# Building the first stage of a projection as a pipeline over feature tiles

## The chip, the cores and the metric

The kernel runs on one core of one Trainium2 chip. The metric is the device time of one execution in microseconds (us), the median of the runs. A core has TensorE (PE: matrix products, with PEld for the loading of their weights), VectorE (DVE), ScalarE (ACT), GpSimd (POOL) and SyncE (SP), which in this kernel issues every DMA transfer. Each engine works off its own list of instructions in order; engines wait for each other by semaphores.

## The reference

Two layers of a diffusion block over 512 tokens (256 latent, 256 context) of 2048 features. The change lies in the head of the even layer, where each token's features are normalised, scaled and shifted, and projected:

```python
shift, scale, gate = jnp.split((s_lat @ ada_w[layer] + ada_b[layer])[:, None, :], 3, axis=-1)   # s_lat = silu(c)
h = rms_norm(x, pre_g[layer]) * (1.0 + scale) + shift
...
hc = rms_norm(ctx, pre_g[layer]) * (1.0 + scale_c) + shift_c      # the same with c_ctx
...
a_v, a_g, b_x, b_b, b_c, b_g = jnp.split(h @ w_in, idx, axis=-1)  # w_in: 2048 x 6144
```

`rms_norm` divides a token by the root of the mean of its squares and multiplies by `pre_g`. So the scale of a feature is a sum over 2048 rows of `ada_w`, and the division by the root is one number per token (called r below), the same for all features. What follows (pooling and convolution, an output projection, the odd layer's gated recurrence) is not touched.

## The kernel before

Features lie on the 128 partitions, 16 feature tiles k of 128 features, and the 512 tokens lie along the free axis, latent and context tokens in the two halves v. A float32 product is made as three products of two-part values: `split` has ScalarE round a value to its high part (L131) and VectorE subtract it for the low part (L132), and `mm3` (L171) issues high x high, high x low and low x high. The low half of a weight, `wlo`, is therefore the last thing that a product waits for.

The first stage makes 7 of the 48 output tiles at once (G0 = 7), one PSUM bank each: `main0(k)` (L337) multiplies a weight of 128x896 (`evg`, 448 KB) by feature tile k into all seven, 21 products of 512 columns, and 16 such passes complete them. Ahead of it the program runs in this order:

- The parameters (L69, 128x344 values, 172 KB) and x, four transfers of 1024 KB (L86), are loaded. ScalarE squares each feature tile of x (L324) and TensorE sums the squares over the partitions (L325, `colsum_mm`); this ends in `r0`, and in `rb0`, r spread over all partitions (`to_rows`).
- The scale columns, silu(c) @ ada_w, are made by TensorE with `col_mm` (L206, products of 32 output rows at L212) from pieces `adaraw` of two 1024 KB transfers each (`ada_raw`, L345), 4 feature tiles to a unit (the first one in two halves of two). VectorE transposes the sums (L230) and `ada_end` adds the bias and multiplies by `pre_g`: `mod`.
- `make_h0` (L352) makes h for a unit's feature tiles: VectorE multiplies x by `mod` and r (L357), ScalarE rounds h to its high half (L360), VectorE makes the low half (L361).

The passes `main0` lie between the units (L376 to L390). The last four lie between the shift columns, of which half is made by TensorE as above and half by VectorE: `ada_dve` (L260) multiplies and sums pieces of a transposed weight, `adat`, of 128x1024 (512 KB) with a row `srow` of silu(c) (loaded and put through SiLU by `load_srow`, L255). `step(n)` does n pieces, two reductions each (L270), one for c and one for c_ctx. `loads` (L115) asks for each piece one step ahead of its use, from a tag `raw2` of two buffers; the weights of the products have a tag `raw` of three, freed by the low half.

After `main0(15)`, `keep` (L408) copies the seven tiles out of PSUM on ScalarE, and `proj_tile` (L176) makes tiles 7 to 11 one at a time, each of two weights of 128x1024 and 48 products, with `step(2)` at each half. All tiles up to the 12th are made of h without the shift; `add_shift` (L413) adds it to h during the last of them, and a bias is made for the tiles that lacked it.

Of the kernel before, what the change touches and what calls it, by code (L numbers as in the profile page):

```python
# [7 lines left out]
F32 = mybir.dt.float32  # L8
# [7 lines left out]
P = 128  # L16
D = 2048
# [30 lines left out]
def block_kernel(ctx: ExitStack, tc: tile.TileContext, par, xt, invcnt, poolw, ada, adat, crow, evg, evb, ev, evo,  # L48
# [36 lines left out]
    for k in range(0, KT, 4):  # L85
        nc.sync.dma_start(xr[k // 8][:, k % 8:k % 8 + 4, :], xt[:, k:k + 4, :])  # L86
# [173 lines left out]
    def ada_dve(units):  # L260

        parts = [(l, t, 4 * u + i, half) for l, t, u in units for i in range(4) for half in range(2)]
        srcs = [adat[ADAT[l, t], n, :, half * 1024:half * 1024 + 1024] for l, t, n, half in parts]
        for (l, t, n, half), raw in zip(parts, loads(srcs)):
            i = n % 4
            if not i and not half:
                sums = a0.tile([P, 2, 4, 2], F32, name="asum", bufs=2)
            for v in range(2):
                junk = a0.tile([P, 1024], BF16, name="ajunk")
                tc.keep_in_program_order(V.tensor_tensor_reduce(  # L270
                    junk, raw, srow[:, v, half * 1024:half * 1024 + 1024], 1.0, sums[:, 0, i, v:v + 1] if half else 0.0,
                    op0=ALU.mult, op1=ALU.add, accum_out=sums[:, half, i, v:v + 1]))
            if half and i == 3:
                ada_end(l, t, n - 3, sums[:, 1])
            yield
# [45 lines left out]
    st0 = aux_ps([P, 1, P], "stps")  # L321
    for k in range(KT):
        sq = tmp512("sq")
        S.activation(sq, xr[k // 8][:, k % 8, :], AF.Square)  # L324
        colsum_mm(st0[:, 0, :], sq, k == 0, k == KT - 1)  # L325
    sxx = cst.tile([P, 4], F32, name="sxx")
    V.tensor_copy(sxx, colsum_end(st0)[:, 0, :])
    r0 = cst.tile([P, 4], F32, name="r0")
    rsqrt_mean(r0, sxx)
# [5 lines left out]


    def main0(k):  # L337

        hh, hl = act0(k)
        whi, wlo = weights()  # L340
        for g in range(G0):
            w = slice(g * P, g * P + P)
            mm3(grp[g], whi[:, w], wlo[:, w], hh, hl, k == 0, k == KT - 1)

# [7 lines left out]
    def make_h0(ks):  # L352
        for k in ks:
            h = xr[k // 8][:, k % 8, :]
            for v in range(2):
                c = slice(v * SEQ, v * SEQ + SEQ)
                V.scalar_tensor_tensor(h[:, c], h[:, c], mod[:, 0, 1, k, v:v + 1], rb0[:, c],  # L357
                                       op0=ALU.mult, op1=ALU.mult)
            hh, hl = act0(k)
            S.copy(hh, h)  # L360
            V.tensor_tensor(hl, h, hh.bitcast(F32), op=ALU.subtract)  # L361


    for t in h0[0] + h0[1]:
        GP.memset(t[:, 0, 0:1].bitcast(F32), 0.0)
    raws = [ada_raw(0, 1, 0, s) for s in range(2)]
    for s in range(2):
        acc = aux_ps([P, 64], "adaps")
        for g in range(4):
            col_mm(acc, s_pad, raws[s][:, g, :], g, 4)  # L370
        ada_pe_end(0, 1, 2 * s, acc)
        if s == 0:
            rb0, _ = to_rows(r0, a0.tile([P, 512], F32, name="rb0", tag="a2k"))
            grp = [mm_ps() for _ in range(5)] + [aux_ps([P, 512], "mmx") for _ in range(G0 - 5)]
        make_h0((2 * s, 2 * s + 1))
    for u in range(1, 4):  # L376
        acc = aux_ps([P, P], "adaps")
        for s in range(2):
            if u == 1 and s == 0:
                main0(0)  # L380
                main0(1)
            if u == 3 and s == 0:
                load_srow()
            raw = ada_raw(0, 1, u, s)
            for g in range(4):
                col_mm(acc, s_pad, raw[:, g, :], 4 * s + g)
            for k in range(2, 4) if (u, s) == (1, 0) else () if u == 1 else range(4 * u - 4 + 2 * s, 4 * u - 2 + 2 * s):
                main0(k)
        ada_pe_end(0, 1, 4 * u, acc)
        make_h0(range(4 * u, 4 * u + 4))  # L390

    job = ada_dve([(0, 0, u) for u in range(2, 4)])

    for u in range(2):
        acc = aux_ps([P, P], "adaps")
        for s in range(2):
            raw = ada_raw(0, 0, u, s)
            for g in range(4):
                col_mm(acc, s_pad, raw[:, g, :], 4 * s + g)
            main0(12 + 2 * u + s)  # L400
            step(1 + u)
        ada_pe_end(0, 0, 4 * u, acc)
# [5 lines left out]
    def keep(i, o):  # L408
        d = pend[i // 8][:, i % 8, :]
        S.copy(d, o)  # L410
        return d

    def add_shift(ks):  # L413
        for k in ks:
            hh, hl = act0(k)
            h = xr[k // 8][:, k % 8, :]
# [6 lines left out]
    done = [keep(i, grp[i]) for i in range(G0)]  # L423
    while len(done) < NPRE - 1:
        t = mm_ps()
        proj_tile(t, act0, lambda half: step(2))
        done.append(keep(len(done), t))
# [771 lines left out]
```

## Time and the profile before

| | |
|---|---|
| median of 3 runs | 1687.82 us (1687.19 to 1688.19) |
| profiled execution, its own time | 1686.03 us |
| its span, first to last instruction | 1684.3 us |
| mean granted clock of TensorE | 0.991 of full speed |
| TensorE busy | 1641.8 us, 97% of the span |
| VectorE busy | 1195.4 us, 71% |
| ScalarE busy | 597.5 us, 35% |
| DMA engines, mean busy share | 53.0% of 16 engines |

Busy time and waits are taken from one profiled execution, so its own time, 1686.03 us, is what they add up to; it lies 1.8 us under the median of the runs. The share of TensorE is an average over all stages. What a change in the first stage does is read from that stage's own stretch of time and from the waits in it.

### The profile page before, as it was taken

The page shows a single profiled execution, that of the slowest core. Times are in us where ns is not written, and L with a number is a line of the kernel's source. Part 1 is how long each engine was busy: PE and PEld are TensorE (multiplying, and loading weights), DVE is VectorE, ACT ScalarE, POOL GpSimd, SP SyncE. Part 2 cuts the span into 40 slices and gives each one's busy share as a digit, 9 for nine tenths or more (in the row PEclk, how much of TensorE's full clock was granted, in tenths as well). Part 3 has the DMA queues.
Part 4 walks back from the last instruction along what each step waited for, and adds up shares of the span by engine and source line. Part 5 has one row for each costly group of instructions (what it writes and reads, how often), then busy time and mean ns, then how long its engine had stood idle before and what let it go on. Part 6 is the DMA issues. An engine that isn't in the chain of part 4 may idle for free.

```text
span 1684.3 us, 23062 instructions
## 1 busy us (share of the span) xinstructions
PE 1641.8 (97%) x8878; PEld 1355.5 (80%) x8878; DVE 1195.4 (71%) x2079; ACT 597.5 (35%) x944; POOL 79.4 (5%) x154
## 2 busy tenths in 40 slices
PE   6999999999999999997999999999999999999997
PEld 4777778888888888885788888888888888888886
DVE  3458977977777778876995863878548773666854
ACT  4323533322222233332443432443334442343543
POOL 0000000000000000004100000000100000000000
PEclk9999999999999999998999999999999999999999
DMA  9987455666665686643376533636325333333453
GB/s 359 354 311 229 162 184 168 195 194 195 190 197 191 194 294 199 199 151 110 91 176 185 184 113 100 211 111 204 121 93 189 118 113 100 120 106 113 175 186 126
DMA packets 98046, 295.28 MB, mean 175 GB/s; under 512 B 26000, under 2 KB 26128, under 8 KB 96272
## 3 DMA queue, kind: packets, MB, share of 16 engines
q1 hardware_dynamic: 97936, 293.82, 53.0%
q8 instruction: 69, 1.13, 0.3%
q14 instruction: 41, 0.34, 0.1%
HBM read 289.58 MB, written 4.19 MB: 174 GB/s over the span
## 4 chain that ended last, share of the span: by engine, by line
PE 91%; DVE 5%; DMA 3%; issue 1%; ACT 0%; POOL 0%; SPq 0%; DVEq 0%; POOLq 0%; ACTq 0%
PE mmps L173 19%; PE mmps L174 19%; PE mmps L172 19%; PE mmps L191 6%; PE mmps L952 3%; PE mmps L954 3%; PE mmps L953 3%; PE mmps L192 3%; DMA adaraw<-ada_dram 1%; PE adaps L212 1%; PE mmps L1060 1%; PE mmps L1061 1%; PE mmps L1059 1%; DVE wlo L132 1%; PE mmx L173 1%
## 5 line engine op out<-in xcount | busy, mean ns | idle before, releaser
L131 ACT CAST whi<-raw 128x1024 fp32r<-128x1024 f32 (+3 forms) x328 | 335.7, 1025 | 842.6 <-PE mmps L173 547.5
L132 DVE TENSOR_TENSOR wlo<-raw,whi 128x1024 fp32r<-128x1024 f32 (+3 forms) x328 | 388.8, 1187 | 291.3 <-ACT whi L131 283.8
L172 PE MATMUL mmps<-h,whi 128*128 128x512 f32 x1216 | 477.9, 394 | 8.0 <-ACT h L710 6.5
L173 PE MATMUL mmps<-h,whi 128*128 128x512 f32 x1216 | 477.0, 392 | 3.8 <-DVE h L711 3.7
L174 PE MATMUL mmps<-h,wlo 128*128 128x512 f32 x1216 | 475.2, 391 | 3.5 <-DVE wlo L132 3.5
L172 PEld LDWEIGHTS mmps<-h,whi 128*128 128x128 f32 x1216 | 229.4, 189 | 59.5 <-ACT h L710 7.1
L174 PEld LDWEIGHTS mmps<-h,wlo 128*128 128x128 f32 x1216 | 229.2, 188 | 53.3 <-DVE wlo L132 4.4
L173 PEld LDWEIGHTS mmps<-h,whi 128*128 128x128 f32 x1216 | 229.8, 189 | 52.1 <-DVE h L711 5.0
L191 PE MATMUL mmps<-h,whi 128*128 128x512 f32 x496 | 177.8, 401 | 0.0
L192 PE MATMUL mmps<-h,wlo 128*128 128x256 f32 x496 | 139.2, 281 | 0.2 <-DVE wlo L132 0.2
L270 DVE CUSTOM_DVE_ANT_0 ajunk<-raw,srow,asum 128x1024 bf16<-128x1024 f32 x104 | 133.2, 1281 | 2.7 <-DMA raw<-adat_dram 1.2
L270 DVE CUSTOM_DVE_ANT_0 ajunk<-raw,srow 128x1024 bf16<-128x1024 f32 x104 | 126.9, 1220 | 2.6 <-DMA raw<-adat_dram 1.5
L191 PEld LDWEIGHTS mmps<-h,whi 128*128 128x128 f32 x496 | 93.1, 188 | 22.9 <-issue 0.5
L952 PE MATMUL mmps<-whi,h 128*128 128x512 f32 x256 | 100.1, 391 | 0.0
L954 PE MATMUL mmps<-wlo,h 128*128 128x512 f32 x256 | 99.8, 390 | 0.0
L953 PE MATMUL mmps<-whi,h 128*128 128x512 f32 x256 | 99.8, 390 | 0.0
L172 PE MATMUL mmps<-yin,whi 128*128 128x512 f32 x256 | 99.6, 389 | 0.0
L173 PE MATMUL mmps<-yin,whi 128*128 128x512 f32 x256 | 99.6, 389 | 0.0
L174 PE MATMUL mmps<-yin,wlo 128*128 128x512 f32 x256 | 99.6, 389 | 0.0
L192 PEld LDWEIGHTS mmps<-h,wlo 128*128 128x128 f32 x496 | 93.6, 189 | 1.2 <-DVE wlo L132 0.5
L954 PEld LDWEIGHTS mmps<-wlo,h 128*128 128x128 f32 x256 | 48.0, 188 | 10.1
L174 PEld LDWEIGHTS mmps<-yin,wlo 128*128 128x128 f32 x256 | 48.0, 188 | 10.1
(271 smaller groups left out, 1967.5 us busy)
## 6 DMA issues: line engine op xcount, KB each, us to landing
raw<-odz_dram SPq DMA_DIRECT2D x118, 512.0 KB, 3.3
raw<-adat_dram SPq DMA_DIRECT2D x104, 512.0 KB, 4.6
raw<-ev_dram SPq DMA_DIRECT2D x82, 512.0 KB, 4.3
adaraw<-ada_dram SPq DMA_DIRECT2D x24, 1024.0 KB, 9.2
raw<-ada_dram SPq DMA_DIRECT2D x36, 512.0 KB, 4.4
raw<-evo_dram SPq DMA_DIRECT2D x32, 512.0 KB, 4.5
raw<-odi_dram SPq DMA_DIRECT2D x32, 512.0 KB, 3.3
raw<-odo_dram SPq DMA_DIRECT2D x32, 512.0 KB, 3.4
```

The source lines that it names most:

```text
L131: S.copy(hi[:, 0:n], raw[:, 0:n])
L132: V.tensor_tensor(lo[:, 0:n], raw[:, 0:n], hi[:, 0:n].bitcast(F32), op=ALU.subtract)
L172: T.matmul(o, whi, xhi, start=first, stop=False)
L173: T.matmul(o, whi, xlo, start=False, stop=False)
L174: T.matmul(o, wlo, xhi, start=False, stop=last)
L191: T.matmul(o, whi, xhl, start=first, stop=False)
L192: T.matmul(o[:, 0:SEQ], wlo, xhl[:, 0, :], start=False, stop=last)
L212: T.matmul(acc[32 * j:32 * j + 32, :], vec[:, k, :], rv[:, i, j, :], start=k == 0, stop=k == KT - 1, tile_position=(0, 32 * j))
L270: tc.keep_in_program_order(V.tensor_tensor_reduce(junk, raw, srow[:, v, half * 1024:half * 1024 + 1024], 1.0, sums[:, 0, i, v:v + 1] if ha ...
L952: T.matmul(o, xh[:, c], hi[:, w], start=k == 0, stop=False)
L953: T.matmul(o, xl[:, c], hi[:, w], start=False, stop=False)
L954: T.matmul(o, xh[:, c], lo[:, w], start=False, stop=k == KT - 1)
```

## The change

The first stage becomes a pipeline over small units of feature tiles: (0), (1), and then pairs (2, 3) to (14, 15). For each feature tile the scale columns have a 1024 KB transfer of their own (`adas`, in longer rows) and x one of 256 KB (`fetch`). h is made of x and `mod` alone, without r (`scale0`); r multiplies the outputs when they are kept (`keep`, now on VectorE), and `norm_job` multiplies x by `mod` and r later, for `add_shift`. The squares are added up on VectorE (`squares`) and summed over partitions once, near the end. The order of the stage is written out by hand (`manual_schedule`: what stands there keeps the order of the code on every engine). The shift columns made by TensorE lie between the last two passes; the steps on VectorE begin three units in, two to a unit, where `load_srow` now stands too.

```diff
-    for k in range(0, KT, 4):
-        nc.sync.dma_start(xr[k // 8][:, k % 8:k % 8 + 4, :], xt[:, k:k + 4, :])
...
-    st0 = aux_ps([P, 1, P], "stps")
-    for k in range(KT):
-        sq = tmp512("sq")
-        S.activation(sq, xr[k // 8][:, k % 8, :], AF.Square)
-        colsum_mm(st0[:, 0, :], sq, k == 0, k == KT - 1)
...
+    one_b = cst.tile([P, KT], F32, name="one_b")
+    V.tensor_scalar(one_b, ada_b[:, 0, 1, :], 1.0, None, op0=ALU.add)
+    ssq = a0.tile([P, 512], F32, name="ssq", tag="a2k")
...
+    def fetch(ks):
+        raw = big_tile([P, 2, D], F32, "adaraw")
+        for i, k in enumerate(ks):
+            nc.sync.dma_start(raw[:, i, :], adas[k])
+        for k in ks:
+            nc.sync.dma_start(xk(k), xt[:, k, :])
+        return raw
+    def scale0(ks, raw):
+        n = len(ks)
+        acc = aux_ps([P, 32 * n], "adaps")
+        rv = raw.rearrange("p n (k j i) -> p n k j i", k=KT, j=4)
+        for i in range(KT):
+            for j in range(4):
+                T.matmul(acc[32 * j:32 * j + 32, :].rearrange("p (n i) -> p n i", n=n), s_pad[:, i, :],
+                         rv[:, 0:n, i, j, :], start=i == 0, stop=i == KT - 1, tile_position=(0, 32 * j))
+        tr = transposed(acc, 32 * n, a0)
+        for i, k in enumerate(ks):
+            m = mod[:, 0, 1, k, :]
+            V.tensor_scalar(m, tr[:, 32 * i:32 * i + 2], one_b[:, k:k + 1], pre_g[:, 0, k:k + 1], op0=ALU.add,
+                            op1=ALU.mult)
+        for i, k in enumerate(ks):
+            m = mod[:, 0, 1, k, :]
+            hh, hl = act0(k)
+            for v in range(2):
+                c = slice(v * SEQ, v * SEQ + SEQ)
+                S.activation(hh[:, c], xk(k)[:, c], AF.Copy, scale=m[:, v:v + 1])
+                V.scalar_tensor_tensor(hl[:, c], xk(k)[:, c], m[:, v:v + 1], hh[:, c].bitcast(F32), op0=ALU.mult,
+                                       op1=ALU.subtract)
+    def squares(ks):
+        for k in ks:
+            sq = tmp512("sq") if k else ssq
+            S.activation(sq, xk(k), AF.Square)
+            if k:
+                V.tensor_tensor(ssq, ssq, sq, op=ALU.add)
...
+    def main0(k, gs=range(G0)):
...
+    def shift0(s, acc, raw):
+        for g in range(4):
+            col_mm(acc, s_pad, raw[:, g, :], 4 * s + g)
...
+    units = [(0,), (1,)] + [(k, k + 1) for k in range(2, KT, 2)]
+    del order[-KT:]
+    first_w = {}
+    with tc.manual_schedule():
+        job = iter(())
+        raws, w_raws = [], []
+        for ks in units[:2]:
+            raws.append(fetch(ks))
+            w_raws.append([load(evg[k]) for k in ks])
+        for i, ks in enumerate(units):
+            prev = units[i - 1] if i else ()
+            if len(prev) == 2:
+                main0(prev[0])
+            elif prev:
+                main0(prev[0], range(4))
+            scale0(ks, raws[i])
+            for k, raw in zip(ks, w_raws[i]):
+                first_w[k] = split(raw, G0 * P)
+            if 0 < i < len(units) - 1:
+                w_raws.append([load(evg[k]) for k in units[i + 1]])
+            if i + 2 < len(units):
+                raws.append(fetch(units[i + 2]))
+            squares(ks)
+            if i == 3:
+                load_srow()
+                job = ada_dve([(0, 0, u) for u in range(2, 4)])
+            if len(prev) == 2:
+                step(2)
+                main0(prev[1])
+            elif prev:
+                main0(prev[0], range(4, G0))
...
+        ahead()
+        acc = aux_ps([P, P], "adaps")
+        raw = [ada_raw(0, 0, 0, s) for s in range(2)]
+        shift0(0, acc, raw[0])
+        raw.append(ada_raw(0, 0, 1, 0))
+        main0(KT - 2)
+        shift0(1, acc, raw[1])
+        raw.append(ada_raw(0, 0, 1, 1))
+        ada_pe_end(0, 0, 0, acc)
+        st0 = aux_ps([P, 1, P], "stps")
+        colsum_mm(st0[:, 0, :], ssq)
+        sxx = cst.tile([P, 4], F32, name="sxx")
+        V.tensor_copy(sxx, colsum_end(st0)[:, 0, :])
+        r0 = cst.tile([P, 4], F32, name="r0")
+        rsqrt_mean(r0, sxx)
+        main0(KT - 1, range(4))
+        rb0, _ = to_rows(r0, a0.tile([P, 512], F32, name="rb0", tag="a2k"))
+        acc = aux_ps([P, P], "adaps")
+        shift0(0, acc, raw[2])
+        main0(KT - 1, range(4, G0))
+        shift0(1, acc, raw[3])
+        ada_pe_end(0, 0, 4, acc)
+        step(1)
+    manual = False
...
-    raws = [ada_raw(0, 1, 0, s) for s in range(2)]
-    for s in range(2):
-        acc = aux_ps([P, 64], "adaps")
-        for g in range(4):
-            col_mm(acc, s_pad, raws[s][:, g, :], g, 4)
-        ada_pe_end(0, 1, 2 * s, acc)
-        if s == 0:
-            rb0, _ = to_rows(r0, a0.tile([P, 512], F32, name="rb0", tag="a2k"))
-            grp = [mm_ps() for _ in range(5)] + [aux_ps([P, 512], "mmx") for _ in range(G0 - 5)]
-        make_h0((2 * s, 2 * s + 1))
...
-        S.copy(d, o)
...
+        V.tensor_tensor(d, o, rb0, op=ALU.mult)
...
+    def norm_job():
+        for k in range(KT):
...
+                V.scalar_tensor_tensor(xk(k)[:, c], xk(k)[:, c], mod[:, 0, 1, k, v:v + 1], rb0[:, c], op0=ALU.mult,
+                                       op1=ALU.mult)
+            if k % 2:
+                yield
...
+    norms = norm_job()
     while len(done) < NPRE - 1:
         t = mm_ps()
-        proj_tile(t, act0, lambda half: step(2))
+        proj_tile(t, act0, lambda half: (step(1), next(norms, None)))
...
-    w = a["ada_w"][0, :, D:D + 512].reshape(4, 4, P, 2, 2, 4, 32)
-    ada[0, 1, 0] = w.transpose(3, 0, 2, 1, 5, 4, 6).reshape(8, P, 1024)
+    adas = a["ada_w"][0, :, D:2 * D].reshape(KT, P, KT, 4 * 32).transpose(2, 1, 0, 3).reshape(KT, P, D)
```

What this makes of the queues is seen in two places. **The first place** is SyncE's list around one unit. Before, around the last unit of scale columns and the first two of shift columns (`raw` is a weight of the products, `raw2` a piece of the reduction, `adaraw` a piece of columns, and a number behind a name tells one buffer's use from the next):

```order
L104 DMA raw_941<-evg_dram 128x896
L348 DMA adaraw_990<-ada_dram 128x2x1024 x2
L104 DMA raw_1025<-evg_dram 128x896
L104 DMA raw2_1052<-adat_dram 128x1024
L104 DMA raw2_1054<-adat_dram 128x1024
L348 DMA adaraw_1061<-ada_dram 128x2x1024 x2
L104 DMA raw_1096<-evg_dram 128x896
L104 DMA raw2_1123<-adat_dram 128x1024
```

And in the changed kernel, SyncE's list over the same unit of work, in the middle of the loop (feature tiles 8 and 9 are fetched after the weights of tiles 6 and 7, and the next unit's weights follow):

```order
L105 DMA raw_694<-evg_dram 128x896
L105 DMA raw_696<-evg_dram 128x896
L350 DMA adaraw_698<-adas_dram 128x2048 x2
L352 DMA xr_70<-xt_dram 128x512 x2
L105 DMA raw2_709<-adat_dram 128x1024
L105 DMA raw2_715<-adat_dram 128x1024
L105 DMA raw_848<-evg_dram 128x896
L105 DMA raw_850<-evg_dram 128x896
```

Before, two pieces of the reduction stand together behind one weight, ahead of the columns; now the pieces `raw2_709` and `raw2_715` stand behind two weights, two transfers of columns and two of x. **The second place** is VectorE's list where the steps of the reduction begin. Before, in the shift units (`ajunk` is the reduction's unused output, `asum` its sums, and the one-column row behind a reduction reads the sum out; the `raw2` in a row tells which piece it needs):

```order
L361 TENSOR_TENSOR h0_196<-xr_70,h0_194 128x512 x2
L132 TENSOR_TENSOR wlo_1028<-raw_1025,whi_1027 128x896
L270 ISA ajunk_1057,asum_1056<-raw2_1052,srow_88 128x1024
...
L270 ISA ajunk_1059,asum_1056<-raw2_1052,srow_88 128x1024
...
L132 TENSOR_TENSOR wlo_1099<-raw_1096,whi_1098 128x896
L270 ISA ajunk_1125,asum_1056<-raw2_1054,srow_88,asum_1056 128x1024
...
L230 STREAM_TRANSPOSE adatr_1129<-adaps_989 128x128
```

And in the changed kernel, VectorE's list from the low halves of tile 6's weight and the next to the transpose for tiles 8 and 9:

```order
L133 TENSOR_TENSOR wlo_687<-raw_533,whi_686 128x896
L133 TENSOR_TENSOR wlo_691<-raw_535,whi_690 128x896
L383 TENSOR_TENSOR ssq_95<-ssq_95,sq_703 128x512
L383 TENSOR_TENSOR ssq_95<-ssq_95,sq_706 128x512
L271 ISA ajunk_711,asum_556<-raw2_561,srow_84 128x1024
...
L271 ISA ajunk_713,asum_556<-raw2_561,srow_84 128x1024
...
L271 ISA ajunk_717,asum_556<-raw2_709,srow_84,asum_556 128x1024
...
L271 ISA ajunk_719,asum_556<-raw2_709,srow_84,asum_556 128x1024
...
L231 STREAM_TRANSPOSE adatr_828<-adaps_763 128x64
L367 TENSOR_SCALAR mod_83<-adatr_828,one_b_93,pt_67 128x2 x2
L375 SCALAR_TENSOR_TENSOR h0_88<-xr_70,mod_83,h0_86 128x256 x4
```

Before, one step lies between two low halves, and no h waits behind it: all of h0 was made ahead of the first step. Now two steps lie ahead of the transpose that h of the next two tiles needs, and the second of them reads `raw2_709`, the piece that stands behind the fetch in SyncE's list above.

## Rows read from the trace of the kernel before

**Rows 1.** The page's top: span, and each engine's busy time, share, instructions.

```profile
span 1684.3 us, 23062 instructions
...
PE 1641.8 (97%) x8878; PEld 1355.5 (80%) x8878; DVE 1195.4 (71%) x2079; ACT 597.5 (35%) x944; POOL 79.4 (5%) x154
```

**Rows 2.** Three windows: length, busy PE/PEld/DVE/ACT/POOL, granted clock, DMA share, GB/s.

```profile
0.00:27.77 27.77, 14.60 (x386) 8.51 (x387) 7.53 (x31) 14.69 (x25) 3.34 (x15) 0.94 0.95 374
27.77:131.04 103.27, 100.74 (x978) 80.32 (x978) 52.05 (x96) 33.29 (x43) 0.53 (x1) 0.98 0.86 325
131.04:200.00 68.96, 65.99 (x282) 53.96 (x283) 66.53 (x124) 29.10 (x53) 0.00 (x0) 0.98 0.60 194
```

**Rows 3.** TensorE in order of time: start, busy us, what, [idle before <-releaser].

```profile
16.69 1.10 PE L212 MATMUL adaps<-adaraw,s_pad 128*32 128x64 f32 x64
...
67.29 0.50 PE L172 MATMUL mmps<-h,whi 128*128 128x512 f32 x1
...
77.03 1.96 PE L212 MATMUL adaps<-adaraw,s_pad 128*32 128x128 f32 x64
...
131.04 0.50 PE L174 MATMUL mmps<-h,wlo 128*128 128x512 f32 x1 [0.53 <-DVE wlo L132]
...
194.73 0.60 PE L174 MATMUL mmps<-h,wlo 128*128 128x512 f32 x1 [2.97 <-DVE wlo L132]
```

**Rows 4.** The chain that ended last, in order of time: start, us, what.

```profile
28.54 0.43 PE mmps L173
...
31.41 0.23 PE mmps L172
```

**Rows 5.** ScalarE in order of time.

```profile
6.53 2.19 ACT L324 ACTIVATE sq<-xr 128x512 f32<-128x512 f32 x4 [0.18 <-DMA xr<-xt_dram]
...
14.10 2.19 ACT L324 ACTIVATE sq<-xr 128x512 f32<-128x512 f32 x4 [0.32 <-DMA xr<-xt_dram]
...
26.69 1.92 ACT L131 CAST whi<-raw 128x896 fp32r<-128x896 f32 x2 [0.62 <-DMA raw<-evg_dram]
...
67.58 1.92 ACT L258 ACTIVATE srow<-srow 128x2048 f32<-128x2048 f32 x1
...
175.70 10.11 ACT L420 ACTIVATE h<-xr,mod 128x256 fp32r<-128x256 f32 x25
```

**Rows 6.** SyncE's waits before 135 us: total us, times, longest.

```profile
SPq L104 <- DVE asum L270: 19.0, 4, 8.4
SPq L104 <- DVE wlo L132: 18.8, 6, 5.4
```

**Rows 7.** VectorE in order of time.

```profile
22.80 0.25 DVE L230 STREAM_TRANSPOSE adatr<-adaps 128x64 f32<-128x64 f32 x1 [3.09 <-PE adaps L212]
...
28.23 0.17 DVE L224 TENSOR_SCALAR mod<-mod 128x4 f32<-128x4 f32 x1
...
32.43 2.09 DVE L132 TENSOR_TENSOR wlo<-raw,whi 128x896 fp32r<-128x896 f32 x2
...
68.39 3.26 DVE L357 SCALAR_TENSOR_TENSOR xr<-xr,mod,rb 128x256 f32<-128x256 f32 x8
...
102.19 1.28 DVE L270 CUSTOM_DVE_ANT_0 ajunk<-raw,srow,asum 128x1024 bf16<-128x1024 f32 x1
```

**Rows 8.** The page's transfers: count, KB each, median us from issue to landing.

```profile
raw<-odz_dram SPq DMA_DIRECT2D x118, 512.0 KB, 3.3
```

**Rows 9.** SyncE's issues in order of time: start, us, transfer, count.

```profile
90.67 1.52 SPq L348 DMA_DIRECT2D adaraw<-ada_dram  x2
...
92.29 0.41 SPq L104 DMA_DIRECT2D raw<-evg_dram  x1
```

**Rows 10.** Landings of transfers issued at 92.29, 103.25 and 101.16 us.

```profile
raw<-evg_dram SPq DMA_DIRECT2D x1, 448.0 KB, 7.6
...
raw<-evg_dram SPq DMA_DIRECT2D x1, 448.0 KB, 11.4
...
raw<-adat_dram SPq DMA_DIRECT2D x1, 512.0 KB, 4.4
```

## What was predicted, before the changed kernel had run

> **What bounds the kernel now.** I read the page first: TensorE is busy 1641.8 us of a span of 1684.3 [rows 1], so a change can only save time where TensorE stands, and costs all that it makes it stand. Next the stages [rows 2]: up to 27.77 us TensorE is busy 14.60 us, on column sums and on the products that make the scale columns; the first product of the projection starts there. From 27.77 to 131.04 it is busy 100.74 of 103.27 us. The two later losses are in its order of time [rows 3]: a wait that ends at 131.04, where the first full-width tile (call it tile 7) gets its weights, and one that ends at 194.73, where VectorE is late with the low half of a weight (2.97 us). The chain shows the clock's two levels by the time one 512-column product takes in it: 0.43 us at 1.2 GHz, 0.23 at 2.4 [rows 4].
>
> In this stage the transfers are the second resource. Four x loads of 1024 KB let the squares start from 6.53 to 14.10 us [rows 5], so 1024 KB per 2.52 us, 406 KB/us. SyncE issues every transfer in the order of the program, and the waits of its queue show what that costs: before 135 us it stood 19.0 us for the reduction of L270 and 18.8 us for low halves of weights [rows 6].
>
> **Start: what is removed.** The squares no longer stand ahead of the products, and 1024 KB of scale columns now serve one feature tile. The first scale product needs parameters (172 KB), the pool's counts (256), and 1024 KB: 1452 KB. The first square before waited for 1196 KB until 6.53 [rows 5]; 256 KB more at 406 make 7.2. 64 products of 32 columns: the row of 32 products with 64 columns (64 records) took 1.10 us [rows 3], so 1.1 to 2.2 at the high level, times 1.9 at the low: I take 2.4, to 9.6. Then the chain of a unit: transpose 0.25, a short operation per tile 0.17, the high halves on ScalarE 0.40 per 256 columns, the cast of a weight 0.96, its low half 1.05 [rows 5, 7]. The first main product (a pass `main0`) starts at about 11.7, **16 us earlier**.
>
> **Up to unit 3 TensorE paces.** A pass of 21 products is half of 77.03 less 67.29, so 4.87 us [rows 3]; a scale product of two tiles, 64 products of 64 columns, is twice 1.10. Unit 0's twelve products at mostly the low level end at 16.3; scale product 1.5, the other nine 2.0; then a wait on unit 1's chain of about 1 us, twelve products, the scale product of tiles 2 and 3 to 25.8, nine products; a wait of 1.6 (one tile gives too little cover for the chain), main product of tile 2, the scale product of 4 and 5 to 36.7. The chain of two tiles, from the end of the scale product to the first low half of a weight, is 0.25 + 0.34 + 4 x 0.40 + 0.96 + 1.05, 4.2 us: the low half of tile 4 stands at 40.9.
>
> **What the change adds: VectorE waits for a transfer that stands behind the fetch.** In the loop, two steps of the reduction stand on VectorE between one unit's weights and the transpose of the next unit's scale columns (second place of the order shown). The second step reads a piece that SyncE issues behind the next weight and the whole fetch (first place). That weight's own buffer is free only when the low half of the unit's first tile is made. So a ring closes: low half, then weight 448 KB, scale columns 2 x 1024, x 2 x 256, piece 512, together 3520 KB; two reductions of 1.28 and their reads, 2.6; chain 4.2; the next low half. TensorE's unit is 2 x 4.87 + 2.2 = 11.9 us, so the ring decides when the landing L exceeds 11.9 - 6.8 = 5.1 us.
>
> No row shows such a group landing. Fixed part: a 512 KB transfer in the calm part lands in 3.3 us [rows 8], less 512/406, so 2.0. Lower bound, at the rate of the x loads: 2.0 + 3520/406 = 10.7. Upper: two 1024 KB loads issued from 90.67 and a weight at 92.29 that lands 7.6 later, 2496 KB in 9.2 us [rows 9, 10], so 349 KB/us: 12.1; the same group at 102 us had its weight only after 11.4, half as long again: about 16.5. The new loads read longer rows, like x, so I take 390 KB/us: **L = 11.1, a ring of 17.9 us**, three times (the units that fetch the sixth to eighth).
>
> The Trainium skill speaks against this change here: "DMA: Bandwidth & Descriptors", in its section on the anatomy of one DMA, has semaphore waits happen on the issuing sequencer before dispatch, and the trace agrees, with the 19.0 us above. Its fit there, 2.0 us and 436 GB/s (given for GpSimd's path), would make an estimated L of 10.3 and a total some 5 us lower; its limit of 358 GB/s of HBM for a core (Specifications) an estimate of 12.1 and 6 us more, but the first 27.77 us ran at a mean of 374 [rows 2], so the measurement decides against that limit.
>
> **The first ring is longer.** In unit 3 the row of c for the reduction comes too: behind the low half of tile 4 (40.9) stand 448 + 2048 + 512 + 2048 KB, so its second copy lands at 41.0 + 2.0 + 5056/390 = 56.0 and the first piece at 57.3. ScalarE's high halves for unit 4 stand behind the two SiLU passes of 1.9 us [rows 5], VectorE's transpose behind four reductions (5.3): 62.6. First weight cast at +3.2, so main product 6 starts at 65.8; TensorE was through with main product 5 at 53.3. It stands **12.5 us**. Low half of tile 6: 66.8. Three rings: tile 12's at 120.5.
>
> **The end of the stage.** Four more reductions and the last chain put the low half of tile 14 at about 132.9. The next pair of reductions frees, at 137.7, a piece buffer whose load stands at the head of SyncE's queue, ahead of a weight and the shift pieces: 512 + 512 + 1024 KB, landing at 145.0, the second half at 147.6. TensorE ended main product 13 at about 133.5 and stands 11.5 us. From 148.5: main product 14 4.9, shift product 2.0 (1.96 in [rows 3]), sums 0.4, twelve products 2.8, the broadcast of r 1.1, shift 2.0, nine products 2.0, shift 2.0: 165.7, and tile 7 at full pace at about 167, against 131.0. **Later by 36 us**, the 16 us at the start included.
>
> **After the stage.** VectorE keeps seven tiles (12 in all, at 0.6 to 0.7 us by the 512-column work before, 8 us) and scales x later (32 x 0.41 [rows 7], 13 us), but has three or four of sixteen reduction parts left, where it had ten (25 us). In this stretch it was busy 66.53 of 68.96 us [rows 2]; it stays full, so the edits are hidden only while weights still come in time. The wait at 194.73 and its products at the low level cost about 4.7 us; I take 2 to 3 of that back, and expect 0 to 3 of new late low halves. Adding squares on VectorE (about 1.3 us a unit) lies inside the landing; if that cover went, it would be 1.3 us per unit. The removed column sums lay under waiting ScalarE: nothing.
>
> **Sum.** 36 - 2 + 1 to 2 = about +36 us. The profiled execution before took 1686.0 (1684.3 of span); with it 1722, and as the median of the runs lies 1.8 above, **1724 us**. Its own range is 1712 to 1736, from L between 10.7 and 12.1 (3 rings, the longer first one and the shift pieces: -3 to +7) and the unknown start and end, 5 each way.
>
> **Rivals.**
> *The pipeline holds* (faster). If the second step's piece were there when VectorE comes to it (L at most 5.1), TensorE alone would pace from 36.7: 13 x 4.87 + 5 x 2.2 + 4 x 1.96 + 1 = 83, so tile 7 at about 121: 10 us earlier, with the later wait 12, 1676. For it: TensorE fills 97% of a stage that has loads of the same total. Against: a piece with nothing ahead of it took 4.4 us [rows 10], and here 3008 KB go ahead. Chance 0.05.
> *Only the row of c stalls.* One stall of 12.5 us and none in the rings: 1676 + 12 = 1688, no change. It needs the same short L from unit 4 on. 0.04.
> *Slow landings.* With 1.5 times the landing, as at 102 us: +5.5 for each of three rings, +7 in the first, +4 at the shift pieces, 1751. 0.11.
> *The low clock level stays.* If TensorE didn't recover within a unit, 42 x 0.43 + 3.8 = 22 us would exceed the ring: +4 for four units, 1740. For it: after the wait that ended at 194.73 the products were slow again, and from 28.54 to past 31 they took 0.43 [rows 3, 4]; against: there they were back at 0.23 after about 3.5 us, and the 5 us that TensorE has to spare in a ring cover the 1.6 us that eight slow products cost. The Trainium skill, "TensorE: Matmul & The Clock Gate", section on HAM oscillation, describes such a kernel that starts cold after every DMA wait; by it each stall costs those 1.6 us, which the ring hides. 0.08.
>
> **How the numbers follow.** Forecast 0.72; the rest as given. Slower by over 0.2% (3.4 us; about what a measurement of this kernel can tell from no change) is the forecast with the last two rivals and a little of the second: 0.91; faster 0.05, same 0.04. The range 1706 to 1748 holds the forecast, the low clock, and part of the slow landings; it leaves out both fast cases and about half of the slow landings.
>
> **What the profile would show.** First main product near 12 us; TensorE idle about 12 us near 53 to 66, 3 to 6 us in each of three units some 18 us apart, and about 11 us ahead of the first shift product; each ended by the cast of a weight, with VectorE waiting about 5 to 7 us for a reduction piece before it. SyncE's longest waits would be for low halves. Wrong would be: units of 12 us, pieces that land within 5 us, or tile 7 before 131.

## The result, and the profile after

The changed kernel takes 1732.75 us (median of 4 runs, 1731.41 to 1736.64) against 1687.51 before: the ratio is 1.0272, with a 95% interval of 1.0254 to 1.029. The profiled execution took 1732.59 us, 46.6 more than the 1686.03 before. The forecast was 1724 with a range of 1706 to 1748.

The page's top shows where such a loss lies. Against [rows 1] TensorE's busy time has grown by 7.6 us and the span by 46.6, so TensorE stands some 39 us more than before:

```profile
span 1730.9 us, 23916 instructions
...
PE 1649.4 (95%) x9270; PEld 1359.7 (79%) x9270; DVE 1219.5 (70%) x2128; ACT 594.1 (34%) x948; POOL 79.2 (5%) x154
```

TensorE in order of time from the first pass on, where it began again after a wait of more than 2 us (the answer to [rows 3]), and the last shift products, after which the first full-width tile runs at full pace:

```profile
12.39 0.76 PE L173 MATMUL mmps<-h,whi 128*128 128x512 f32 x1 [2.56 <-ACT whi L132]
...
67.98 0.80 PE L173 MATMUL mmps<-h,whi 128*128 128x512 f32 x1 [12.18 <-ACT whi L132]
...
87.52 0.79 PE L173 MATMUL mmps<-h,whi 128*128 128x512 f32 x1 [5.70 <-ACT whi L132]
...
106.87 0.80 PE L173 MATMUL mmps<-h,whi 128*128 128x512 f32 x1 [5.07 <-ACT whi L132]
...
127.79 0.80 PE L173 MATMUL mmps<-h,whi 128*128 128x512 f32 x1 [6.12 <-ACT whi L132]
...
154.51 1.94 PE L213 MATMUL adaps<-adaraw,s_pad 128*32 128x128 f32 x32 [12.13 <-DMA adaraw<-ada_dram]
...
178.02 1.08 PE L213 MATMUL adaps<-adaraw,s_pad 128*32 128x128 f32 x32
179.03 0.50 PE L175 MATMUL mmps<-h,wlo 128*128 128x512 f32 x1
```

The first pass starts at 12.39 us where it started at 27.77 before, and the first full-width tile at 179 where it started at 131. Between lie one stall of 12.18 us, three of 5 to 6, and one of 12.13. The releaser of four of them is the cast of a weight, but that is only the last link. The chain that ended last, through one of the short stalls (start, us, what), shows the whole ring:

```profile
87.50 1.10 DVE wlo L133
...
88.62 0.33 SPq L105
...
89.04 0.38 SPq L350
...
90.42 0.47 SPq L352
...
90.94 10.07 DMA raw<-adat_dram
...
101.14 1.28 DVE ajunk L271
...
102.47 1.28 DVE ajunk L271
...
103.77 0.17 DVE adatr L231
...
105.10 0.89 ACT h L374 x2
105.99 0.84 ACT whi L132
...
106.85 1.10 DVE wlo L133
```

Read it downwards: a low half ends, SyncE issues the weight that had waited for it, then the fetch and the piece; the piece lands; two reductions; transpose, high halves, cast; and the next unit's low half, 19.35 us later. TensorE does not stand in this stretch of the chain: it is not what paces these units. VectorE's waits for the piece in those three rings, and SyncE's longest waits before 200 us (the answer to [rows 6]; total us, times, longest):

```profile
81.74 1.28 DVE L271 CUSTOM_DVE_ANT_0 ajunk<-raw,srow,asum 128x1024 bf16<-128x1024 f32 x1 [7.87 <-DMA raw<-adat_dram]
...
101.14 1.28 DVE L271 CUSTOM_DVE_ANT_0 ajunk<-raw,srow,asum 128x1024 bf16<-128x1024 f32 x1 [7.74 <-DMA raw<-adat_dram]
...
121.86 1.29 DVE L271 CUSTOM_DVE_ANT_0 ajunk<-raw,srow,asum 128x1024 bf16<-128x1024 f32 x1 [9.10 <-DMA raw<-adat_dram]
```

```profile
SPq L105 <- DVE wlo L133: 75.5, 13, 15.2
SPq L105 <- DVE asum L271: 41.7, 11, 12.9
```

SyncE's 75.5 us for low halves look like the larger loss and are not a cause of their own: in the first and the eleventh run below it still waits 63.6 and 62.1 us for them, and the ring is gone.

### The profile page after: what moved, and what is told of

Same layout as the page of the kernel before. It is cut to its first block, busy times and chain, and to the rows that moved or that the text cites. A ratio compares the mean times of both kernels' runs of the same rounds, so it can differ in the third digit from the quotient of the medians.

```text
span 1730.9 us, 23916 instructions
## 1 busy us (share of the span) xinstructions
PE 1649.4 (95%) x9270; PEld 1359.7 (79%) x9270; DVE 1219.5 (70%) x2128; ACT 594.1 (34%) x948; POOL 79.2 (5%) x154
## 4 chain that ended last, share of the span: by engine, by line
PE 83%; DVE 5%; DMA 4%; issue 2%; ACT 1%; SPq 0%; POOL 0%; DVEq 0%; POOLq 0%; ACTq 0%
PE mmps L174 17%; PE mmps L173 17%; PE mmps L175 17%; PE mmps L192 6%; PE mmps L1012 3%; PE mmps L1014 3%; PE mmps L1013 3%; PE mmps L193 3%; DMA raw<-evb_dram 1%; DMA raw<-adat_dram 1%; PE mmps L1121 1%; PE mmps L1120 1%; PE mmps L1119 1%; DVE wlo L133 1%; DVE h L480 1%
## 5 line engine op out<-in xcount | busy, mean ns | idle before, releaser
L250 DVE SCALAR_TENSOR_TENSOR rest<-raw,s_pad,rest 128x512 f32<-128x512 f32 x60 | 45.0, 749 | 15.9 <-DMA raw<-ada_dram 15.1
```

What stands on the lines that cost most here:

```text
L250: V.scalar_tensor_tensor(acc[:, v, :], w, sc, acc[:, v, :], op0=ALU.mult, op1=ALU.add)
```

## The experiments

Each run is of a whole kernel, and its ratio is to the kernel before on the same chip. Only the seventh and the last scale x with other instructions, and the eighth to tenth do work that nothing reads; the rest compute the same in another order or with other buffers.

Differences of one or two us between runs should not be read closely, for two reasons. The runs were made on several chips, on which the kernel before took 1686.15 to 1687.59 us. And the runs that add a pool of buffers (1, 3, 5 to 10 and 12) also ask for `inv`, 256 KB that the pooling needs, after 115 us in place of at 1.24 us. Their first pass starts at 10.72 to 11.39 us, that of the changed kernel and of runs 2, 4 and 11 at 12.34 to 13.95. Little of this is left at the end of the first stall (66.47 to 68.02 us in runs 1, 8, 9 and 10, 67.98 in the changed kernel), but runs 5, 6, 7 and 12 have no such stall and may keep it.

| run | median us | ratio, 95% interval |
|---|---|---|
| changed kernel | 1732.75 | 1.0272 (1.0254 to 1.029) |
| 1 pieces three ahead | 1706.07 | 1.0113 (1.0098 to 1.0128) |
| 2 no steps in the loop | 1709.03 | 1.0132 (1.0116 to 1.0148) |
| 3 five weight buffers | 1706.40 | 1.0116 (1.01 to 1.0132) |
| 4 shift columns early | 1727.88 | 1.0234 (1.0214 to 1.0253) |
| 5 run 1, row of c later | 1690.38 | 1.0019 (1.0008 to 1.0031) |
| 6 run 5, shift columns and weight early | 1679.27 | 0.9955 (0.9943 to 0.9967) |
| 7 run 6, x scaled on ScalarE and GpSimd | 1686.26 | 0.9996 (0.9987 to 1.0005) |
| 8 changed, 3 extra transfers | 1739.84 | 1.0309 (1.0292 to 1.0326) |
| 9 run 1, 3 extra transfers | 1707.07 | 1.0124 (1.0106 to 1.0142) |
| 10 changed, squares added twice | 1732.89 | 1.0273 (1.0258 to 1.0288) |
| 11 changed, one piece ahead of the fetch | 1711.29 | 1.0137 (1.0123 to 1.0152) |
| 12 run 6, x scaled on ScalarE and VectorE | 1681.90 | 0.9963 (0.995 to 0.9977) |

**1. Is it the piece behind the fetch?** `loads` keeps four buffers and asks three pieces ahead:

```diff
+        q = []
+        for n, src in enumerate(srcs):
+            q.append(load(src, "raw2", 2, s0 if deep and n % 4 > 1 else wp))
+            if len(q) == (4 if deep else 2):
+                yield q.pop(0)
+        yield from q
```

> The changed kernel, with the reduction pieces of this stage in four buffers and asked for three ahead, so that the piece a unit's second step reads was issued a unit earlier. Theory (the piece that lands behind the fetch paces the units): the three stalls of 5.70, 5.07 and 6.12 us go, the units from tile 6 on take about 12 us in place of 19.5, 19.4 and 20.9; the first stall of 12.2 stays, up to 2 us longer for the one piece more behind the row of c. 3 x 7.5 = 22 us less: 1708 to 1714. Rival A (SyncE's wait for low halves of weights paces, with or without the pieces): the units stay at 17 us and more, 1728 to 1735. Rival B (the transfers of a unit need the 12.7 us that they took, whatever waits for them): units of 13 to 15 us, 1715 to 1722. Rival C (VectorE's own work, 5.3 us of reductions a unit, is too much): the units stay at 16 us and more with VectorE busy between.

Measured: 1706.07 us, 27 less than the changed kernel and 1.9 under the expected range: the three rings gave back 24.1 us, the unit behind them 1.2. The low halves of the pairs from tile 6 on, VectorE in order of time:

```profile
67.84 2.10 DVE L132 TENSOR_TENSOR wlo<-raw,whi 128x896 fp32r<-128x896 f32 x2 [0.34 <-ACT whi L131]
...
80.04 2.09 DVE L132 TENSOR_TENSOR wlo<-raw,whi 128x896 fp32r<-128x896 f32 x2 [0.30 <-ACT whi L131]
...
91.70 2.09 DVE L132 TENSOR_TENSOR wlo<-raw,whi 128x896 fp32r<-128x896 f32 x2 [0.34 <-ACT whi L131]
...
103.56 2.10 DVE L132 TENSOR_TENSOR wlo<-raw,whi 128x896 fp32r<-128x896 f32 x2 [0.35 <-ACT whi L131]
```

The units are 12.2, 11.7 and 11.9 us apart, TensorE's own pace. SyncE still waits 63.6 us for low halves (rival A falls), VectorE does the same reductions (C falls), and the same bytes are moved (B falls). The first stall is 14.10 us and the one at the shift columns 12.97.

**2. The steps out of the loop.** `step(2)` is deleted there, and the hook at each half tile does two steps in place of one:

```diff
-                step(2)
                 main0(prev[1])
...
-        proj_tile(t, act0, lambda half: (step(1), next(norms, None)))
+        proj_tile(t, act0, lambda half: (step(2), next(norms, None)))
```

> The changed kernel without the two steps of the reduction in each unit; they run behind the stage, two at each half tile in place of one. The row of c is still loaded at the fourth unit. Theory: no stall from the units of tiles 8, 10 and 12; a first stall stays, since ScalarE's high halves for tile 6 still stand behind the two passes over the row of c (the second ended at 60.1), shorter by the reductions of 59.61 to 64.88: about 7 us in place of 12.2. The first full-width tile 25 us or more earlier than 179; behind it VectorE has 12 more pieces, 31 us, in a stretch in which it is busy 19 of 20 us: 1705 to 1722, by how much of that the later tiles hide. Rival A (low halves of weights): the stalls stay without the steps, 1730 and more. Rival that the stage is not the loss but VectorE's load behind it (keeping of tiles, x scaled late): slower than the changed kernel.

Measured: 1709.03. There is no stall in the units of tiles 8 to 12, and none at the shift columns either, since no piece stands at the head of SyncE's queue there. The first stall is 8.21 us. Behind the stage five waits of 1.74 to 3.90 us for low halves, 14.8 in all, give part of it back: the reductions cost there what they did not cost in run 1.

**3. Five buffers for the weights** (`load(evg[k])` from two pools in turn).

> The changed kernel with five buffers for this stage's weights in place of three, pieces as they were: SyncE no longer stands at a weight until a low half is made, so the fetch and the pieces behind it go out earlier. Theory: what the second step waits for is then issued at the first step of the unit before, 12 to 13 us of landing within a ring over two units, so the units run at 12 us: about 20 us less, 1708 to 1716; the first stall, a matter of bytes behind the row of c, shrinks by some 5 us at most. Rival B (the transfers' own time): units of 13 to 15 us, 1715 to 1722. If the wait for low halves only shifts to the piece's own buffer, units of 16 us and more: 1725 to 1733.

Measured: 1706.40, 1.6 under the expected range; units of 14.7, 13.2, 13.7 and 11.7 us, first stall 8.80. The units were longer than the 12 us of the theory, and the first stall ended 6.6 us sooner than in the changed kernel, where at most 5 were expected. The ring can be cut at this link too, with the piece still behind the fetch; but part of SyncE's wait shifts to the pieces' own buffers (59.0 us for the reduction, 15.3 for low halves).

**4. The shift columns early**: `ada_raw` for the first two is called in the last two units, behind `scale0`, which frees its buffer.

> The changed kernel, with the first two pairs of transfers of shift columns issued in the last two units, ahead of those units' pieces, in place of behind them. Theory: the stall of 12.1 us ahead of the first shift product goes; but the second unit from the end now has 2048 KB ahead of its pieces again, so that its 1.0 us of waiting (units of 12.9 us) becomes a ring like the others, 17 to 19 us. Net 5 to 7 us less: 1725 to 1728. Rival (the shift stall is one of transfer rate, not of order): 1731 to 1734.

Measured: 1727.88, and both halves of the expectation are seen: the unit from tile 12 to 14 grew from 12.9 to 17.0 us, and the first shift product waits no more. But another wait took its place. TensorE's order of time, and VectorE's just before:

```profile
159.67 0.66 PE L287 MATMUL stps<-ssq,ones 128*32 128x128 f32 x8 [6.31 <-DVE adatr L231]
```

```profile
158.16 1.23 DVE L133 TENSOR_TENSOR wlo<-raw,whi 128x1024 fp32r<-128x1024 f32 x1 [3.87 <-ACT whi L132]
159.31 0.31 DVE L231 STREAM_TRANSPOSE adatr<-adaps 128x128 f32<-128x128 f32 x1
```

The transpose was ready and stood behind the low half of the first full-width tile's weight, whose transfer now comes last.

**5. The row of c later**: run 1, and `load_srow` split into its transfer (units four and five) and its SiLU (unit six); the first three pieces are asked for in unit five, the first step is done in unit six, so that the loop holds 8 steps in place of 12.

> The deeper pieces of the first run, and also the row of c asked for in halves of 1024 KB in the fourth and fifth unit, its two SiLU passes and the first reductions only in the sixth, and the first three pieces asked for in the fifth (8 steps in the loop in place of 12). Theory: the first stall was the row of c in ScalarE's list ahead of the high halves, and its pieces in VectorE's, so it goes, 14.1 us in the run with deep pieces; low halves every 11.7 to 12.2 us from 40 us on; the 13 us ahead of the first shift product stay: 1692 to 1695. Rival B (the bytes of these units are the limit, 4544 KB with half of the row, 11.7 us at 390 KB/us and 13.3 at the 342 that the rings showed): stalls of 1 to 4 us in two units, 1695 to 1700.

Measured: 1690.38, 15.7 less than run 1. It is more than expected: no stall over 1 us is left between 28 us and the shift columns; the one there is 13.27 us.

**6. All three**: run 5 with the shift columns early, as in run 4, and the first full-width tile's weight asked for in the last unit.

> The run before, and the shift columns asked for in the last two units, and the weight of the first full-width tile in the last unit ahead of its pieces (in the run with early shift columns TensorE still stood 6.3 us behind a low half on VectorE that waited for that weight). Theory: no stall over 2 us ahead of the first full-width tile, which starts 8 to 10 us before the 129.8 of the kernel before; behind it VectorE is as full as in the kernel before (66.5 of 69 us) with the keeping and scaling of x added, so that at most half of this stays: 1682 to 1687. Rival (VectorE behind the stage gives all of it back): 1687 to 1691.

Measured: 1679.27, 0.45% faster than the kernel before and better than expected. TensorE, all waits of over 1.1 us from the first pass to 200 us:

```profile
10.82 0.77 PE L174 MATMUL mmps<-h,whi 128*128 128x512 f32 x1 [2.56 <-ACT whi L133]
...
110.00 1.08 PE L214 MATMUL adaps<-adaraw,s_pad 128*32 128x128 f32 x32 [1.12 <-DMA adaraw<-ada_dram]
...
132.28 0.50 PE L176 MATMUL mmps<-h,wlo 128*128 128x512 f32 x1 [2.15 <-DVE wlo L134]
```

The first full-width tile starts at 122.23 us, where it started at 129.78 before and was at full pace at 131.04 [rows 3]:

```profile
122.23 0.50 PE L174 MATMUL mmps<-h,whi 128*128 128x512 f32 x1 [0.19 <-DVE pend L481]
```

The same pipeline, with the awaited transfers issued a unit or more ahead of the instructions that wait for them, keeps about half of what it gained at the start: 17 us there, 8.8 at the first full-width tile, 8.1 at the end. From the first pass to that tile TensorE is busy 105.61 of 111.41 us (before, 100.74 of 103.27 [rows 2]), and the DMA engines are busy 0.98 of the time, so that this stage has little room left.

**7. Less for VectorE behind the stage**: in `norm_job`

```diff
-                V.scalar_tensor_tensor(xk(k)[:, c], xk(k)[:, c], mod[:, 0, 1, k, v:v + 1], rb0[:, c], op0=ALU.mult,
-                                       op1=ALU.mult)
+                S.activation(xk(k)[:, c], xk(k)[:, c], AF.Copy, scale=mod[:, 0, 1, k, v:v + 1])
+            GP.tensor_tensor(xk(k), xk(k), rb0, op=ALU.mult)
```

> The run before, with the late scaling of x by mod on ScalarE and by r on GpSimd, 13 us less on VectorE behind the stage. If VectorE is the bound there: 3 to 6 us less than the run before, 1678 to 1683. If it is not, or if GpSimd's passes over 512 columns slow VectorE's or come too late for the shift to be added: the same or slower, 1683 to 1690.

Measured: 1686.26, 7 slower than run 6: the second of the two cases. GpSimd's passes, and VectorE's work beside them and after them:

```profile
117.40 26.79 POOL L489 TENSOR_TENSOR xr<-xr,rb 128x512 f32<-128x512 f32 x16 [2.85 <-ACT rb L323]
```

```profile
131.89 2.27 DVE L134 TENSOR_TENSOR wlo<-raw,whi 128x1024 fp32r<-128x1024 f32 x1
134.09 2.29 DVE L277 CUSTOM_DVE_ANT_0 ajunk<-raw,srow,asum 128x1024 bf16<-128x1024 f32 x1
...
146.95 1.21 DVE L134 TENSOR_TENSOR wlo<-raw,whi 128x1024 fp32r<-128x1024 f32 x1
148.09 1.27 DVE L277 CUSTOM_DVE_ANT_0 ajunk<-raw,srow,asum 128x1024 bf16<-128x1024 f32 x1
```

While GpSimd works, these two kinds of instruction take nearly twice as long on VectorE, eight of them together some 8.5 us more.

**8 to 10. Doses.** One transfer of 1024 KB more behind three fetches, in the changed kernel (run 8, into two buffers) and in run 1 (run 9, into one); and the squares added twice in the changed kernel (run 10).

```diff
+            if i in (4, 5, 6):
+                nc.sync.dma_start(s0.tile([P, D], F32, name="extra", bufs=2), adas[i])
...
                 V.tensor_tensor(ssq, ssq, sq, op=ALU.add)
+                V.tensor_tensor(sqx, sqx, sq, op=ALU.add)
```

> The changed kernel with one more transfer of 1024 KB, which nothing reads, behind the fetch of the fifth, sixth and seventh unit, ahead of the reduction pieces. Theory (landing, reductions, chain and low half make a ring): each of the three rings of 19.5, 19.4 and 20.9 us grows by the transfer's time, 2.6 us at 390 KB/us to 3.1 at 330, so 8 to 10 us in all: 1740 to 1743. Rival (the units are paced by something beside the transfers, with room in them: VectorE, the clock, SyncE's wait for low halves): less than 3 us more, 1732 to 1736.

> The kernel with deep pieces (1706.1 before) with the same three transfers. Theory: nothing waits for the piece behind the fetch, units of 11.7 to 12.2 us have room for 4544 KB at 390 KB/us (11.7 us) but little more: 0 to 5 us more, 1706 to 1711, against 8 to 10 in the kernel with the ring. If the transfers themselves set the pace in both, 8 us or more here too: 1714 and above.

> The changed kernel with the squares added up on VectorE twice, the second time into a tile that nothing reads, 1.3 us more per unit ahead of the first reduction. Theory: VectorE waits 7.7 to 9.1 us for the second step's piece in a ring, so this work lies in the wait: within 2 us of the changed kernel, 1731 to 1735. Rival C (VectorE's own work paces the units): 1.3 us in each of four to seven units, 1738 to 1742.

Measured: 1739.84, 1707.07 and 1732.89. In the changed kernel the transfers cost 7.1 us (just below the 8 to 10 expected), and the low halves stand where they should:

```profile
67.05 2.09 DVE L133 TENSOR_TENSOR wlo<-raw,whi 128x896 fp32r<-128x896 f32 x2 [0.34 <-ACT whi L132]
...
88.89 2.09 DVE L133 TENSOR_TENSOR wlo<-raw,whi 128x896 fp32r<-128x896 f32 x2 [0.29 <-ACT whi L132]
...
110.78 2.09 DVE L133 TENSOR_TENSOR wlo<-raw,whi 128x896 fp32r<-128x896 f32 x2 [0.34 <-ACT whi L132]
...
134.61 2.09 DVE L133 TENSOR_TENSOR wlo<-raw,whi 128x896 fp32r<-128x896 f32 x2 [0.34 <-ACT whi L132]
```

The three rings are 21.8, 21.9 and 23.8 us in place of 19.5, 19.4 and 20.9: 7.8 us for 3072 KB, 396 KB/us. With deep pieces the same transfers cost 1.0 us, within the spread of the runs. The profiled execution of run 9, the slowest of its four (1711.04 us), has more: from the low half of tile 6 to that of tile 14 it takes 50.8 us where run 1 took 47.4. And 1.3 us more of VectorE's work per unit cost 0.1 us, because in a ring it lies ahead of a wait.

**11. Only the place of one transfer.** From the fifth unit on, one piece is issued ahead of the fetch (`pulls[0]()` in front of `fetch(units[i + 2])`); buffers and transfers are those of the changed kernel.

> The changed kernel with one thing moved: from the fifth unit on, the piece that the unit's second step reads is issued behind the weights and ahead of the fetch, in place of behind it; the same transfers, the same two buffers. Theory (its place behind 2560 KB of fetch makes the ring): if transfers land in their order, the piece lands some 2.0 + 960/396 = 4.4 us after the first low half, under the 5.1 at which TensorE paces, so units of about 12 us: 1707 to 1711. If all that is in flight shares the rate evenly, the piece takes 6 to 8 us and units are 13 to 15 us: 1712 to 1722. Rival A (SyncE's wait for low halves): 1728 to 1735 as before. The first stall and that of the shift columns stay.

Measured: 1711.29, 21 less than the changed kernel. The second step's wait, and the next low half:

```profile
75.35 1.28 DVE L278 CUSTOM_DVE_ANT_0 ajunk<-raw,srow,asum 128x1024 bf16<-128x1024 f32 x1 [1.48 <-DMA raw<-adat_dram]
...
81.12 2.09 DVE L140 TENSOR_TENSOR wlo<-raw,whi 128x896 fp32r<-128x896 f32 x2 [0.35 <-ACT whi L139]
```

The low half before ended at 69.0, so the piece landed in 6.3 us in place of 12.7, and the units are 13.2, 12.6, 13.1 and 12.2 us. The place is shown to be the cause. How the transfers share the way is less clear: 6.3 us is what an even share was expected to give (6 to 8), not the 4.4 of transfers that land in their order, but only two of the four units lie in the 13 to 15 us of that case, and the total lies 0.7 us under its 1712 to 1722.

**12. x scaled on ScalarE and VectorE**, run 7 with `V.tensor_tensor` in place of `GP.tensor_tensor`.

> The kernel with all three repairs (1679.3 before), with x scaled by mod on ScalarE and by r on VectorE over 512 columns, 16 passes of 0.69 us in place of 32 of 0.41 to 0.48: 3 us less on VectorE behind the stage, no GpSimd. If the loss of the GpSimd version (1686.3) was GpSimd's passes slowing VectorE's (2.27 us for a low half in place of 1.22 while they ran), this one is within 3 us of 1679.3: 1676 to 1681. If it was the scaling of x on ScalarE, ahead of its casts, this one loses too: 1683 to 1687.

Measured: 1681.90, which cannot be told from run 6. It is out of the first range by 0.9 and 1.1 under the second; most of run 7's loss (4.4 of 7.0 us) came from GpSimd beside VectorE, and a small one from ScalarE's part is not excluded.

## Why the prediction was right

**Direction, place and mechanism** were right, and shown: runs 1, 3 and 11 cut or shorten the ring at three different links, and run 8 lengthens it by the transfers' own time. **The start** was forecast at 11.7 us and is 12.39. **The first stall** was forecast at 12.5 and is 12.18, but the lengths agree by luck: TensorE came to it at 55.8 us in place of 53.3 and left it at 68.0 in place of 65.8. The first piece landed 2.3 us later than the 57.3 of the forecast:

```profile
59.61 1.23 DVE L271 CUSTOM_DVE_ANT_0 ajunk<-raw,srow 128x1024 bf16<-128x1024 f32 x1 [15.02 <-DMA raw<-adat_dram]
```

Runs 2 and 5 part its two causes: with the steps gone 8.21 us are left for the row of c in ScalarE's list, and run 5 removes it. **The stall at the shift columns** was forecast at 11.5 and is 12.13; it comes from the piece at the head of SyncE's queue, for it is gone where there is no such piece (run 2) and where the shift columns are issued ahead of it (run 4).

**The term that was mis-sized is L.** The forecast was 46.6 - 36 = 10.6 us short. First stall 2.2, three rings of 59.8 us in place of 53.7: 6.1, the unit behind them 0.5, the landing of the shift columns 0.7, the way from the first shift product to the full-width tile 24.5 us in place of 22: 2.5, together 12.0; and behind the stage 1.4 us came back. Part of the 2.5 is the low clock level behind the stall, which the forecast left out there: 32 records of a shift product took 1.94 us at 154.51 and 1.08 us at 178.02. L was 12.7, 12.5 and 13.9 us (from the low half's end to the second step) in place of 11.1, above the forecast's own bounds of 10.7 to 12.1; that the total still lies in the 1712 to 1736 that came from these bounds is owed to the 5 us each way for the start and the end, without which the upper end is 1731. The step that failed was "together 3520 KB": it counted what is issued ahead of the piece. What moved in the 12.7 us of the first ring:

```profile
DMA packets 1073, 4.38 MB, mean 344 GB/s; under 512 B 109, under 2 KB 109, under 8 KB 816
```

3520 KB are 3.60 MB, so 0.78 MB of the next piece and the next weight, issued 2.4 and 2.8 us behind it, had gone by when it landed. At the 396 KB/us of the doses these are 1.9 us, and L would have been 2.0 + 8.9 + 1.9 = 12.8. Run 11 agrees: 6.3 us, not 4.4, for a piece with only a weight ahead of it. That the bytes behind a piece delay it is inferred from these two counts; no run takes them away. The Trainium skill leaves room for it ("DMA: Bandwidth & Descriptors", section on two DMAs through the same engine): descriptors of one queue start in order but are pipelined, and nothing orders transfers across the 16 engines. The third ring's further 1.2 us lie partly in SyncE, whose first two issues of the fetch took 1.77 us in it and 0.86 in the others; why, stays open.

**The page's limit.** The prediction set aside the Trainium skill's 358 GB/s for a core (the same page, Specifications). Run 6 moved more over a long stretch, from 80 to 120 us:

```profile
DMA packets 4223, 16.20 MB, mean 405 GB/s; under 512 B 358, under 2 KB 358, under 8 KB 3961
```

So here the measurement decides, and the estimate of 12.1 that came from that limit was nearer to L for another reason, the bytes behind the piece.

**Behind the stage** the forecast of hidden edits held: 1.4 us came back, and the wait of 2.97 us that ended at 194.73 [rows 3] has no like up to 240 us. **Adding the squares** at no cost was right in the ring (run 10).

**The rivals.** That the pipeline holds, or that only the row of c stalls, needed a piece landing within 5.1 us; it took over 12. With the ring and the other two stalls removed, run 6 comes near the first one's price: the first full-width tile at 122.2 us and 1679.27, where the rival had 121 (its terms add up to 120) and 1676. Slow landings of 1.5 times did not come, but 1.13 to 1.25 did. The low clock was there in each ring (mean granted clock 0.85, 0.85 and 0.83) and did not pace it. Two windows (length, busy PE/PEld/DVE/ACT/POOL, granted clock, DMA share, GB/s), the second ring and the unit behind the third:

```profile
87.52:106.87 19.35, 14.28 (x170) 10.88 (x170) 10.67 (x20) 4.42 (x9) 0.00 (x0) 0.85 0.64 238
...
127.79:140.00 12.21, 12.21 (x161) 9.48 (x162) 10.44 (x19) 3.76 (x8) 0.00 (x0) 0.78 0.51 167
```

With a mean granted clock of 0.85 TensorE was still idle for 5.1 of 19.35 us. In the last window it was busy throughout at 0.78, so that there, once, the slower products behind a stall were on the path: 12.9 us where run 1's units took 11.7 to 12.2.

## What to carry to other kernels

In an order written by hand, a wait for a transfer holds everything behind it on that engine. Follow each transfer back to what lets it be issued: if that is the output of work that stands behind the wait, the loop is a ring, and its length is the landing time and the chain, whatever the engines' loads are. Ask for each transfer one unit ahead of its use (two more buffers gave 27 us here, moving one transfer 21 with none), and count what is issued behind an awaited transfer as well, for here it seems to have shared the way.

## What the runs showed of the hardware

GpSimd's sixteen passes over 128x512 (1.7 us each) made VectorE's low halves take 2.27 us in place of 1.22 and its reductions 2.29 in place of 1.28; the pass that reads PSUM and multiplies by r took 0.68 to 0.69 us with or without them. The Trainium skill ("SBUF — State Buffer", section on who interferes with whom) has the two engines share a pair of ports under an exclusive lock, which fits. So taking 13 us of VectorE's work away in this manner made the kernel 7 us slower than run 6.
